# A hybrid token mixer whose projections run as matmuls of 512 columns, with PSUM handed out in pairs

## Chip, cores and metric

One NeuronCore of a Trainium2 chip (trn2). The time is device microseconds for one execution of the whole program. Of the kernel before, three runs are shown: median 2222.65 us, from 2222.18 to 2224.79 us. The profile is of one further execution, which took 2221.16 us.

## What is computed

Two layers over 256 latent tokens and 256 context tokens of width 1024, all in fp32. Cut to what matters here:

```python
for l in range(2):
    # half-step SwiGLU feed-forward (inner width 2816) on latent and context tokens
    x  = add_residual(x,  swiglu(modulate(x)),  0.5); xc = add_residual(xc, swiglu(modulate(xc)), 0.5)
    h, hc = modulate(x), modulate(xc)                 # RMSNorm, scale, shift
    rq, rk, rv, rg, dq, dk, dv, gates = split(h @ w_in)   # 8192 columns; the same for hc
    ret  = groupnorm(retention(rq, rk, rv)) * silu(rg)          # 4 heads, chunks of 128, state from context
    a    = softmax(dq1 @ dk1.T / 8) - lam * softmax(dq2 @ dk2.T / 8)  # 8 heads, keys of context and latent
    diff = rmsnorm(a @ dv) * (1 - lam_init)
    y    = (sigmoid(gates_a) * ret + sigmoid(gates_b) * diff) @ w_out
    x = add_residual(x, y, 1.0)       # the context too, except in the last layer
    # second half-step feed-forward, like the first; in the last layer for the latent tokens alone
```

The queries and keys of the latent tokens are rotated by position first. In the last layer the context needs no queries, gates or output, only keys and values.

## The kernel before

**Three matmuls for one.** Each large operand is kept as a high part (rounded to the short fp32r form) and a low part (the rest). `mm3` (lines 288 to 291) makes a product of them with three TensorE matmuls: high by high, high by low, low by high. A weight piece of 128x1024 arrives by DMA in a `raw` buffer (4 of them, issued in order by SP). `split` (lines 113 to 118) makes the parts: ScalarE casts the high one (line 116), VectorE subtracts for the low one (line 117), into one of five `w` buffers. The modulation weights (`ada`) are multiplied on VectorE (line 134), during the feed-forwards.

**The mixer** (line 397) takes the 8192 columns of `w_in` in 32 blocks of 256. A block's weights fill two `w` buffers. Rotated queries and keys are made with channels on partitions (`projT_c`, line 471: the weights stand in the array, 256 tokens of one condition stream past), everything else with tokens on partitions (`proj_c`, line 445: 128 tokens stand, 256 channels stream). "Condition" is latent (`LAT`) or context (`CTX`); each has 256 tokens. So every one of these matmuls has 256 columns and each PSUM bank takes two of them.

**The attention** is a generator (`diff_attn`, line 580) run in steps beside the projections. A step makes a score: four matmuls (lines 594 and 595), VectorE maxima (596), ScalarE exponentials (602), VectorE reciprocal, scaling and difference (605 to 609). Two steps later the result is transposed on TensorE (621), copied by ScalarE (623) and multiplied by the values (626). Retention (`ret_head`, line 681) runs the same way. `tick` (line 422) says how many steps follow each projection, `need` (line 433) drains a generator.

**What sets the order.** Each engine runs its instructions in one order, which a scheduler fixes when the program is built, from the order of the code and the readiness that it assumes. TensorE waits where the next instruction's data are late, even if later ones could run. PSUM is 8 banks of 512 columns, each a tile of its own, handed out in turn (`Ring`, line 54). A second ring has 15 SBUF slots of 4 KB per partition.

Of the kernel before, what the change touches and what calls it, by code (L numbers as in the profile page):

```python
# [29 lines left out]
LAG = 2  # L30


def build(ctx, tc, a):
# [8 lines left out]
    adap = ctx.enter_context(tc.tile_pool(name="adap", bufs=4))  # L42
# [25 lines left out]
    banks = Ring(psp, "ps", 8)  # L68
    slots = Ring(rp, "r", 15)

    def bank():
        return banks.get([P, 512])
# [32 lines left out]
    def load(src, halves=(0, 1), pl=rawp, nm="raw"):  # L105
        rs = []
        for j in halves:
            r = pl.tile([P, 1024], F32, tag=nm, name=nm)
            nc.sync.dma_start(r, src[:, j * 1024:(j + 1) * 1024])
            rs.append(r)  # L110
        return rs
# [16 lines left out]
    def ada_gen(l, m, out, conds):  # L128
        for u in range(4):
            r = load(a["wada"][l, m * 4 + u], pl=adap, nm="ada")  # L130
            for j in range(2):
                for c in conds:
                    junk = jp.tile([P, D], BF16, tag="jd", name="jd")
                    dve.tensor_tensor_reduce(  # L134
                        out=junk, in0=r[j], in1=cs[c],
                        scale=1.0, scalar=0.0, op0=ALU.mult, op1=ALU.add,
                        accum_out=out[:, c, 2 * u + j:2 * u + j + 1])
            yield
# [258 lines left out]
    def mixer(l, st, AB, fetch, after):  # L397
# [7 lines left out]
        o, y, M = {}, {}, {}  # L405
# [35 lines left out]
        def proj_w(b):  # L441
            r = load(a["win"][l, b])
            return [split(r[0]), split(r[1])]

        def proj_c(ws, c, ev):
            b0 = bank()
            bk = b0.rearrange("p (j n) -> p j n", j=2)
            for j in range(2):
                t = 2 * c + j
                for k in range(KD):  # L450
                    wt = ws[k // 4].rearrange("p s (k n) -> p s k n", k=4)
                    mm3(bk[:, j], h[k // 2][:, k % 2, 0, t * P:(t + 1) * P], h[k // 2][:, k % 2, 1, t * P:(t + 1) * P],
                        wt[:, 0, k % 4], wt[:, 1, k % 4], k == 0, k == KD - 1)
            flush()
            post = ev(c, bk)
            banks.put(b0)
# [4 lines left out]
        def proj(b, pairs, ev):  # L461
            ws = proj_w(b)
            for c in pairs:
                proj_c(ws, c, ev)

        def projT(b, pairs, ev):
            ws = proj_w(b)
            for c in pairs:
                projT_c(ws, c, ev)

        def projT_c(ws, c, ev):
            b0 = bank()
            bk = b0.rearrange("p (j n) -> p j n", j=2)
            cs_ = slice(c * 256, (c + 1) * 256)
            for j in range(2):
                js = slice(j * P, (j + 1) * P)
                for k in range(KD):
                    wt = ws[k // 4].rearrange("p s (k n) -> p s k n", k=4)
                    mm3(bk[:, j], wt[:, 0, k % 4, js], wt[:, 1, k % 4, js], h[k // 2][:, k % 2, 0, cs_],
                        h[k // 2][:, k % 2, 1, cs_], k == 0, k == KD - 1)  # L480
            flush()
            ev(c, bk)
# [36 lines left out]
        def ev_V(dst):  # L519
            def ev(c, b):  # L520
                nc.scalar.copy(dst[:, 2 * c:2 * c + 2, :], b)
            return ev

        def ev_V2(H, Lo):
            def ev(c, b):
                nc.scalar.copy(H[:, 2 * c:2 * c + 2, :], b)
                dve.tensor_tensor(out=Lo[:, 2 * c:2 * c + 2, :], in0=b, in1=H[:, 2 * c:2 * c + 2, :], op=ALU.subtract)
# [52 lines left out]
        def diff_attn(u, KH, KL, Q, dv):  # L580
            lag = deque()

            def score(c, k0, NK, t, hh):
                if c == LAT:
                    sbk = [bank(), bank()]
                    sb = sbk
                else:
                    b0 = bank()
                    sbk = [b0]
                    sb = [b0[:, 0:256], b0[:, 256:512]]  # L590
                mx = small(2, "mx")
                for m in range(2):
                    qs = Q[m][:, hh, t * P:(t + 1) * P]
                    mm(sb[m], lhsT=qs, rhs=KH[m][:, hh, k0:k0 + NK], start=True, stop=False)  # L594
                    mm(sb[m], lhsT=qs, rhs=KL[m][:, hh, k0:k0 + NK], start=False, stop=True)  # L595
                    dve.reduce_max(mx[:, m:m + 1], sb[m], axis=AX.X)  # L596
# [4 lines left out]
                for m in range(2):  # L601
                    act(e[:, m, :NK], sb[m], AF.Exp, bias=nb[:, m:m + 1], scale=0.125, accum_out=se[:, m:m + 1])  # L602
                banks.put(*sbk)
# [11 lines left out]
            def weigh(c, k0, NK, tt, hh, e):  # L615
# [9 lines left out]
                for i in range(NK // P):  # L625
                    mm(ob[:, tt, hh * P:(hh + 1) * P], lhsT=aT[:, i * P:(i + 1) * P],  # L626
                       rhs=dv[:, k0 // P + i, hh * P:(hh + 1) * P], start=i == 0, stop=i == NK // P - 1)
# [7 lines left out]
                if u not in o:  # L635
                    o[u] = slot([P, 4, 256])
                for tt in range(2):
                    for hh in range(2):
                        dve.scalar_tensor_tensor(out=o[u][:, 2 * c + tt, hh * P:(hh + 1) * P],
# [16 lines left out]
            slots.put(*KH, *KL, *Q, dv)  # L656
# [24 lines left out]
        def ret_head(hd, W, gnb, kk, qq, vv):  # L681
            hl = hd % 2
            for c in QP:
# [20 lines left out]
                if hd not in y:  # L704
                    y[hd] = slot([P, 4, 256])
                yt = y[hd]
                y0 = bank()
                yb = y0.rearrange("p (i n) -> p i n", i=2)
                for i in range(2):
                    for n, j in enumerate(kt):  # L710
                        an = AT[n // 2][:, :, n % 2, i * P:(i + 1) * P]
                        mm3(yb[:, i], an[:, 0], an[:, 1], vv[0][:, j], vv[1][:, j], n == 0, n == len(kt) - 1)
                st = small(12, "bst").rearrange("p (i s) -> p i s", i=2)
                mv = small(4, "bmv").rearrange("p (i s) -> p i s", i=2)
                for i in range(2):
# [6 lines left out]
                    dve.scalar_tensor_tensor(out=yt[:, t, :], in0=yb[:, i],  # L722
# [4 lines left out]
            slots.put(*vv)  # L727
            if hl:
                slots.put(*kk, *qq)

        def ev_gB(u):
            def ev(c, b):
                th = tmp2([P, 2, 256])
                act(th, b, AF.Tanh, scale=0.5)
                oc = o[u][:, 2 * c:2 * c + 2]
# [3 lines left out]
        def ev_rg(hd):  # L739
            def ev(c, b):  # L740
                th = tmp2([P, 2, 256])
                act(th, b, AF.Tanh, scale=0.5)
                dve.scalar_tensor_tensor(out=th, in0=th, scalar=1.0, in1=b, op0=ALU.add, op1=ALU.mult)
                for j in range(2):
                    t = 2 * c + j
                    ys = y[hd][:, t]
                    dve.scalar_tensor_tensor(out=ys, in0=ys, scalar=gr[:, t, hd:hd + 1],
                                             in1=th[:, j], op0=ALU.mult, op1=ALU.mult)
            return ev

        def ev_gA(u):
            def ev(c, b):
                th = tmp2([P, 2, 256])
                act(th, b, AF.Tanh, scale=0.5)
                dve.scalar_tensor_tensor(out=th, in0=th, scalar=1.0, in1=y[u][:, 2 * c:2 * c + 2], op0=ALU.add, op1=ALU.mult)
                dve.tensor_tensor(out=th, in0=th, in1=o[u][:, 2 * c:2 * c + 2], op=ALU.add)

                def post():
                    t0 = bank()
                    tb = t0.rearrange("p (k n) -> p k n", k=2)  # L760
                    for j in range(2):
                        for z in range(2):
                            nc.tensor.transpose(tb[:, z, j * P:(j + 1) * P], th[:, j, z * P:(z + 1) * P], ident)
                    for z in range(2):
                        mt = M[2 * u + z]
                        mH = mt[:, 0, c * 256:(c + 1) * 256]
                        nc.scalar.copy(mH, tb[:, z])
                        dve.tensor_tensor(out=mt[:, 1, c * 256:(c + 1) * 256], in0=tb[:, z], in1=mH, op=ALU.subtract)
                    banks.put(t0)
# [3 lines left out]
        def diff_blocks(u):  # L773
# [239 lines left out]
```

## Time and profile before

| | before |
|---|---|
| median of three runs | 2222.65 us |
| the profiled execution's own time | 2221.16 us |
| its span, first to last instruction | 2219.4 us |
| TensorE matmul busy | 2171.0 us (98%) |
| VectorE busy | 1381.9 us (62%) |
| ScalarE busy | 863.1 us (39%) |

Matmul records overlap: each lasts from its first column to the modelled end of its drain, and the next one starts before. So a matmul's cost in a dense stretch is read from the distance of two starts, not from the duration of a record. Idle time is counted only where no matmul record covers it. The mixers run from about 408 to 928 us and from about 1662 to 2014 us; the rest is feed-forward, a start of some 55 us, and norms.

### The profile page before, as it was taken

To read this page: it belongs to the slowest core of one execution; us is meant where nothing else is said; L and a number is where in the kernel's file an instruction comes from. 1 tells how busy PE (TensorE), PEld (TensorE's weight loads), DVE (VectorE), ACT (ScalarE), POOL (GpSimd) and SP (SyncE) were. 2 spreads that over 40 slices of the span, in tenths; PEclk is the share of its full clock that TensorE was granted. 3 is DMA by queue.
4 is the path that set the end of the run, shared out by engine and by line. 5 is a ranking of instruction groups with operands and counts; after the bars stand their busy time and mean duration, and the time that the engine had idled before them with its cause. 6 is when DMAs were issued, how large, how long until landed. Compare 5 with 4: busy or idle time off the path is not lost. (4 is left out here: it accounts for less than half of the span.)

```text
span 2219.4 us, 32920 instructions
## 1 busy us (share of the span) xinstructions
PE 2171.0 (98%) x13286; PEld 1932.7 (87%) x13286; DVE 1381.9 (62%) x2240; ACT 863.1 (39%) x1379; POOL 127.6 (6%) x245
## 2 busy tenths in 40 slices
PE   7999999999999999999999999999999999998998
PEld 4888888899999999888888888888879999997997
DVE  3899442777767664588234269844348777767554
ACT  3322232645355433432223252223236545445443
POOL 1000000200100010200000020000011010001000
PEclk9999999999999999999999999999999999999999
DMA  8677332122122223266223227853213322345553
GB/s 338 216 253 254 132 121 97 68 70 80 66 77 77 80 85 117 76 209 218 97 102 134 95 92 254 296 184 116 102 57 113 107 84 103 132 152 184 187 184 133
DMA packets 85417, 307.33 MB, mean 138 GB/s; under 512 B 10208, under 2 KB 10416, under 8 KB 85264
## 3 DMA queue, kind: packets, MB, share of 16 engines
q1 hardware_dynamic: 82224, 295.87, 38.1%
q0 software_dynamic: 2752, 8.31, 1.3%
q8 instruction: 104, 1.70, 0.3%
q10 hardware_dynamic: 288, 1.05, 0.1%
q14 instruction: 49, 0.40, 0.1%
HBM read 304.10 MB, written 1.09 MB: 138 GB/s over the span
## 5 line engine op out<-in xcount | busy, mean ns | idle before, releaser
L117 DVE TENSOR_TENSOR w<-raw,w 128x1024 fp32r<-128x1024 f32 x408 | 497.7, 1222 | 462.6 <-ACT w L116 461.5
L289 PE MATMUL ps<-h,w 128*128 128x256 f32 (+1 forms) x2176 | 716.9, 331 | 3.7 <-DVE h L254 2.9
L291 PE MATMUL ps<-h,w 128*128 128x256 f32 (+1 forms) x2176 | 717.3, 330 | 0.4 <-DVE w L117 0.4
L290 PE MATMUL ps<-h,w 128*128 128x256 f32 (+1 forms) x2176 | 717.5, 330 | 0.0
L116 ACT CAST w<-raw 128x1024 fp32r<-128x1024 f32 x408 | 427.5, 1052 | 684.7 <-PE ps L291 613.3
L289 PEld LDWEIGHTS ps<-h,w 128*128 128x128 f32 x2176 | 412.1, 190 | 43.2 <-DVE h L254 4.0
L291 PEld LDWEIGHTS ps<-h,w 128*128 128x128 f32 x2176 | 412.8, 190 | 41.0 <-issue 2.5
L290 PEld LDWEIGHTS ps<-h,w 128*128 128x128 f32 x2176 | 413.3, 190 | 40.1 <-DVE w L117 0.8
L289 PE MATMUL ps<-w,h 128*128 128x256 f32 x1088 | 308.8, 284 | 0.0
L290 PE MATMUL ps<-w,h 128*128 128x256 f32 x1088 | 308.1, 283 | 0.0
L291 PE MATMUL ps<-w,h 128*128 128x256 f32 x1088 | 307.8, 283 | 0.0
L134 DVE CUSTOM_DVE_ANT_0 jd<-ada,r 128x1024 bf16<-128x1024 f32 x224 | 273.6, 1221 | 15.4 <-DMA ada<-wada_dram 10.4
L289 PEld LDWEIGHTS ps<-w,h 128*128 128x128 f32 x1088 | 208.7, 192 | 0.4
L290 PEld LDWEIGHTS ps<-w,h 128*128 128x128 f32 x1088 | 208.7, 192 | 0.3
L291 PEld LDWEIGHTS ps<-w,h 128*128 128x128 f32 x1088 | 208.6, 192 | 0.0
L289 PE MATMUL ps<-w,gs 128*128 128x512 f32 x504 | 196.2, 389 | 0.0
L290 PE MATMUL ps<-w,gs 128*128 128x512 f32 x504 | 196.1, 389 | 0.0
L291 PE MATMUL ps<-w,gs 128*128 128x512 f32 x504 | 196.1, 389 | 0.0
L315 ACT ACTIVATE t<-ps 128x512 f32<-128x512 f32 (+1 forms) x88 | 47.9, 544 | 253.2 <-PE ps L291 249.8
L316 DVE TENSOR_TENSOR r<-ps,t 128x512 f32<-128x512 f32 (+1 forms) x88 | 54.7, 622 | 95.3 <-PE ps L291 69.6
L289 PEld LDWEIGHTS ps<-w,gs 128*128 128x128 f32 x504 | 94.6, 188 | 19.8
L290 PEld LDWEIGHTS ps<-w,gs 128*128 128x128 f32 x504 | 94.6, 188 | 19.6
(169 smaller groups left out, 2164.6 us busy)
## 6 DMA issues: line engine op xcount, KB each, us to landing
raw<-fin_dram SPq DMA_DIRECT2D x176, 512.0 KB, 4.2
ada<-wada_dram SPq DMA_DIRECT2D x128, 512.0 KB, 4.8
raw<-win_dram SPq DMA_DIRECT2D x128, 512.0 KB, 3.5
raw<-fout_dram SPq DMA_DIRECT2D x88, 512.0 KB, 3.5
r<-wada_dram SPq DMA_DIRECT2D x16, 512.0 KB, 10.2
raw<-wout_dram SPq DMA_DIRECT2D x16, 512.0 KB, 3.6
r<-scr POOLq DMA_DIRECT2D x10, 512.0 KB, 4.7
r<-cc_dram SPq DMA_DIRECT2D x7, 512.0 KB, 5.1
```

The costliest lines, as they stand in the source:

```text
L116: keep(nc.scalar.copy(w[:, 0, :], src))
L117: keep(dve.tensor_tensor(out=w[:, 1, :], in0=src, in1=w[:, 0, :], op=ALU.subtract))
L134: dve.tensor_tensor_reduce(out=junk, in0=r[j], in1=cs[c], scale=1.0, scalar=0.0, op0=ALU.mult, op1=ALU.add, accum_out=out[:, c, 2 * u + j: ...
L289: mm(o, lhsT=wH, rhs=xH, start=start, stop=False)
L290: mm(o, lhsT=wH, rhs=xL, start=False, stop=False)
L291: mm(o, lhsT=wL, rhs=xH, start=False, stop=stop)
L315: act(sg[:, :N], ab[0][:, :N], AF.Silu)
L316: dve.tensor_tensor(out=g[f // 2][:, f % 2, :N], in0=ab[1][:, :N], in1=sg[:, :N], op=ALU.mult)
```

## The change

The blocks become 12 of 256 columns with channels on partitions (`winT`) and 10 of 512 columns with tokens on partitions (`winW`). `projT` takes both conditions in one matmul of 512 columns, into two neighbouring banks; `wide` streams 512 channels past 128 tokens, so that it needs four `w` buffers at once. PSUM is one tile; `Banks` hands out single banks or pairs. A latent score takes a pair, and one instruction takes its two maxima. The modulation weights lose their own four buffers and use the slot ring, now 19. `ret_decay` moves into the generator. The stage order is written anew: values of heads 0 and 1 first, then keys and queries of two attention blocks one after the other.

```diff
+    def two(self): ...  # a pair of neighbouring banks; one(): a single one, of an opened pair
-    banks = Ring(psp, "ps", 8)
-    slots = Ring(rp, "r", 15)
+    banks = Banks()
+    slots = Ring(rp, "r", 19)
...
-            r = load(a["wada"][l, m * 4 + u], pl=adap, nm="ada")
+            r = [slot([P, D]) for _ in range(2)]
...
-        def proj_c(ws, c, ev):
-            b0 = bank()
-            bk = b0.rearrange("p (j n) -> p j n", j=2)
-            for j in range(2):
-                t = 2 * c + j
-                for k in range(KD):
-                    wt = ws[k // 4].rearrange("p s (k n) -> p s k n", k=4)
-                    mm3(bk[:, j], h[k // 2][:, k % 2, 0, t * P:(t + 1) * P], h[k // 2][:, k % 2, 1, t * P:(t + 1) * P],
-                        wt[:, 0, k % 4], wt[:, 1, k % 4], k == 0, k == KD - 1)
+        def tok(ws, t, ev):
+            bk = bank()
+            for k in range(KD):
+                wt = ws[k // 2].rearrange("p s (k n) -> p s k n", k=2)
+                mm3(bk, h[k // 2][:, k % 2, 0, t * P:(t + 1) * P], h[k // 2][:, k % 2, 1, t * P:(t + 1) * P],
+                    wt[:, 0, k % 2], wt[:, 1, k % 2], k == 0, k == KD - 1)
+            flush()
+            post = ev(t, bk)
...
+        def wide_w(i):
+            return [split(r) for r in load(a["winW"][l, i], range(4))]
...
+            ws = [split(r) for r in load(a["winT"][l, b])]
+            n = 256 * len(pairs)
+            if len(pairs) == 2:
+                b0 = banks.two()
...
+                    mm3(bk[:, j], wt[:, 0, k % 4, js], wt[:, 1, k % 4, js], h[k // 2][:, k % 2, 0, 0:n],
+                        h[k // 2][:, k % 2, 1, 0:n], k == 0, k == KD - 1)
...
+            for c in pairs:
+                ev(c, bk[:, :, c * 256:(c + 1) * 256])
...
-                    sbk = [bank(), bank()]
+                    b0 = banks.two()
...
-                    dve.reduce_max(mx[:, m:m + 1], sb[m], axis=AX.X)
+                dve.reduce_max(mx, sb, axis=AX.X)
...
+        ws = wide_w(4)
+        for t in range(2):
+            tok(ws, t, ev_V(dv))
+        norm_pair(CTX, AB, h)
+        for t in range(2, 4):
+            tok(ws, t, ev_V(dv))
+        K.update(mixer_consts())
+        kq = diff_blocks(0)
+        diff_defer(0, kq, dv, pick(5, 4))
+        kq = diff_blocks(1)
+        diff_defer(1, kq, dv, pick(6, 5))
+        need("d0")
         rkq_blocks(0)
-        need("d0")
-        diff_blocks(1)
-        gB_block(0)
-        rv_block(0)
+        rv_block(0, pick(4, 2), pick(8, 5))
         need("d1")
-        rv_block(1)
-        gB_block(1)
+        wide(8, QP, ev_gB(0))
+        kq = diff_blocks(2)
...
```

The scheduler makes a new order of it. Three places are shown.

**TensorE, layer 0, first attention block, before.** L594 and L595 are a score's matmuls, L289 to L291 a projection's, L621 the transposition of the first score.

```order
L594 MATMUL ps_3603<-r_3047,r_3051 128x512
L595 MATMUL ps_3603<-r_3049,r_3051 128x512
L594 MATMUL ps_3623<-r_3046,r_3050 128x512
L595 MATMUL ps_3623<-r_3048,r_3050 128x512
...
L289 MATMUL ps_3644<-h,w 128x256
L290 MATMUL ps_3644<-h,w 128x256
L291 MATMUL ps_3644<-h,w 128x256
...
L594 MATMUL ps_3708<-r_3047,r_3051 128x512
L595 MATMUL ps_3708<-r_3049,r_3051 128x512
L621 MATMUL ps_3696<-ident,t_3613 128x128 x4
```

**The same place in the change** (L635 and L636 are the score's matmuls, L328 to L330 the projection's, L662 the transposition).

```order
L635 MATMUL ps<-r_3201,r_3287 128x512
L636 MATMUL ps<-r_3203,r_3287 128x512
L636 MATMUL ps<-r_3202,r_3286 128x512
...
L329 MATMUL ps<-h,w 128x512
L330 MATMUL ps<-h,w 128x512
L328 MATMUL ps<-h,w 128x512
...
L635 MATMUL ps<-r_3200,r_3286 128x512
...
L662 MATMUL ps<-ident,t_3408 128x128 x4
```

Between the last matmul of the first score and its transposition stood 48 projection matmuls of 256 columns and 8 score matmuls; now 14 of 512 columns and 7 score matmuls stand there.

**TensorE, layer 1, first attention block, in the change**, from the first score's last matmul.

```order
L636 MATMUL ps<-r_12477,r_12561 128x512
L635 MATMUL ps<-r_12474,r_12560 128x512
...
L329 MATMUL ps<-h,w 128x512
L330 MATMUL ps<-h,w 128x512
L328 MATMUL ps<-h,w 128x512
...
L662 MATMUL ps<-ident,t_12678 128x128 x4
```

Here 5 projection matmuls and 8 score matmuls are left between the two; before it were 48 and 8, as in layer 0.

**VectorE, start of the mixer in layer 0, in the change.** L317 and L323 are the last residual of the feed-forward, L153 the low parts of weights, L275 the context's norm.

```order
L317 TENSOR_TENSOR t_2956<-ps,r_2743 128x512
L153 TENSOR_TENSOR w<-raw,w 128x1024
L317 TENSOR_TENSOR t_2960<-ps,r_2743 128x512
L323 SCALAR_TENSOR_TENSOR X_107<-t_2956,pr,X_107 128x512
L323 SCALAR_TENSOR_TENSOR X_107<-t_2960,pr,X_107 128x512
L153 TENSOR_TENSOR w<-raw,w 128x1024 x2
L275 TENSOR_SCALAR t_3052<-X_106,pr 128x1024
```

VectorE's order here is as before; but the last two low parts now belong to the first block on TensorE, where before they belonged to the second.

## Rows read from the trace of the kernel before

**Rows 1.** The page's line of engines: busy us, share of the span, instructions.

```profile
PE 2171.0 (98%) x13286; PEld 1932.7 (87%) x13286; DVE 1381.9 (62%) x2240; ACT 863.1 (39%) x1379; POOL 127.6 (6%) x245
```

**Rows 2.** The page's 40 slices of the span (55 us each): busy share in tenths, and TensorE's granted clock in tenths.

```profile
PE   7999999999999999999999999999999999998998
DVE  3899442777767664588234269844348777767554
PEclk9999999999999999999999999999999999999999
```

**Rows 3.** Matmuls of the whole span grouped by line and shape: busy us, mean ns of a record, idle time before them and its releaser. `mm3` issues one of L289, L290, L291 each; `ps<-h,w` streams `h`, `ps<-w,h` streams weights.

```profile
L289 PE MATMUL ps<-h,w 128*128 128x512 f32 x960 | 373.9, 389 | 0.0
L289 PE MATMUL ps<-h,w 128*128 128x256 f32 x1216 | 343.3, 285 | 3.7 <-DVE h L254 2.9 <-ACT t L251 0.6 <-DVE adaA L921 0.2
L289 PE MATMUL ps<-w,h 128*128 128x256 f32 x1088 | 308.8, 284 | 0.0
```

**Rows 4.** TensorE in order of time, in a projection of the mixer: start us, duration us. The rows left out are 45 more of the same three lines.

```profile
641.71 0.28 PE L289 MATMUL ps<-w,h 128*128 128x256 f32 x1
641.82 0.28 PE L290 MATMUL ps<-w,h 128*128 128x256 f32 x1
...
647.34 0.28 PE L291 MATMUL ps<-w,h 128*128 128x256 f32 x1
```

**Rows 5.** TensorE in order of time, in a feed-forward: start us, duration us. The rows left out are 43 more.

```profile
299.68 0.39 PE L289 MATMUL ps<-w,gs 128*128 128x512 f32 x1
299.91 0.39 PE L290 MATMUL ps<-w,gs 128*128 128x512 f32 x1
...
309.88 0.39 PE L289 MATMUL ps<-w,gs 128*128 128x512 f32 x1
```

**Rows 6.** TensorE's waits in the attention, whole span, grouped by line and shape (columns as in group 3).

```profile
L621 PE MATMUL ps<-ident,t 128*128 128x128 f32 x160 | 25.0, 274 | 3.5 <-DVE t L609 3.4
L626 PE MATMUL ps<-r,t 128*128 128x128 f32 x320 | 45.5, 284 | 1.5 <-ACT t L623 1.0
```

**Rows 7.** Busy us of each engine in stretches: a feed-forward, and the first attention block of either layer's mixer. Columns: stretch in us, its length; busy us and instructions of PE, PEld, DVE, ACT, POOL; mean granted clock, DMA's busy share, GB/s.

```profile
100.00:150.00 50.00, 50.00 (x223) 41.29 (x222) 49.45 (x82) 12.60 (x14) 0.53 (x1) 1.00 0.73 250
450.00:500.00 50.00, 48.93 (x386) 46.51 (x385) 38.44 (x89) 21.76 (x53) 2.44 (x4) 1.00 0.19 64
1700.00:1750.00 50.00, 49.33 (x397) 47.78 (x396) 43.27 (x88) 26.75 (x47) 2.17 (x3) 1.00 0.25 87
```

**Rows 8.** Start of the mixer in layer 0, in order of time: TensorE, then VectorE. In brackets the idle time before it and its releaser.

```profile
408.18 0.39 PE L291 MATMUL ps<-w,r 128*128 128x512 f32 x1
408.40 0.28 PE L289 MATMUL ps<-h,w 128*128 128x256 f32 x1
416.50 0.63 PE L247 MATMUL ps<-ident,t 128*128 128x128 f32 x4 [0.86 <-DVE t L236]
426.40 0.51 PE L289 MATMUL ps<-h,w 128*128 128x256 f32 x2 [1.78 <-DVE h L254]
...
412.53 2.35 DVE L117 TENSOR_TENSOR w<-raw,w 128x1024 fp32r<-128x1024 f32 x2
419.78 0.75 DVE L236 TENSOR_SCALAR t<-X,pr 128x1024 f32<-128x1024 f32 x1
425.92 0.43 DVE L254 CAST h<-t 128x512 fp32r<-128x512 f32 x1 [1.68 <-ACT t L251]
```

**Rows 9.** TensorE, layer 0, first attention block: the last matmul of the first score, and the transpositions of the first and the fourth.

```profile
454.88 0.40 PE L595 MATMUL ps<-r,r 128*128 128x512 f32 x1
...
462.92 0.66 PE L621 MATMUL ps<-ident,t 128*128 128x128 f32 x4
...
473.56 0.60 PE L621 MATMUL ps<-ident,t 128*128 128x128 f32 x4
```

**Rows 10.** TensorE, a later attention block: the last matmul of its first score and that score's transposition.

```profile
640.56 0.40 PE L595 MATMUL ps<-r,r 128*128 128x512 f32 x1
...
647.46 0.60 PE L621 MATMUL ps<-ident,t 128*128 128x128 f32 x4
```

**Rows 11.** VectorE from 405 to 2040 us, grouped by line and shape (columns as in group 3).

```profile
L117 DVE TENSOR_TENSOR w<-raw,w 128x1024 fp32r<-128x1024 f32 x284 | 346.1, 1221 | 314.5 <-ACT w L116 313.5
L491 DVE TENSOR_TENSOR t<-ps,dtab 32x512 f32<-32x512 f32 x64 | 44.0, 687 | 1.0
L596 DVE TENSOR_REDUCE mx<-ps 128x1 f32<-128x512 f32 x64 | 42.0, 682 | 10.4 <-PE ps L595 10.3
L608 DVE TENSOR_SCALAR t<-t,rc 128x512 f32<-128x512 f32 x32 | 15.4, 480 | 0.0
L609 DVE SCALAR_TENSOR_TENSOR t<-t,r 128x512 f32<-128x512 f32 x32 | 24.0, 749 | 0.8
L663 DVE TENSOR_SCALAR gnb<-gnb 128x256 f32<-128x256 f32 x8 | 2.3, 289 | 7.9 <-DMA gnb<-gnw_dram 7.9
```

**Rows 12.** ScalarE's cast of weights, same stretch and columns.

```profile
L116 ACT CAST w<-raw 128x1024 fp32r<-128x1024 f32 x284 | 297.1, 1051 | 458.3 <-PE ps L291 413.8 <-issue 33.6 <-DVE adag L134 4.4
```

**Rows 13.** Stretches around TensorE's longest idle time, in the last layer between mixer and feed-forward (columns as in group 7).

```profile
2016.00:2020.00 4.00, 0.00 (x0) 0.00 (x0) 3.01 (x5) 3.20 (x9) 3.56 (x6) 0.91 0.39 133
2020.00:2024.00 4.00, 1.78 (x7) 1.41 (x8) 2.46 (x3) 0.00 (x0) 2.28 (x3) 0.50 0.35 114
2024.00:2028.00 4.00, 4.00 (x27) 3.94 (x27) 2.60 (x6) 3.75 (x8) 0.00 (x0) 0.74 0.06 24
```

More of the change, by code (lines that the diff above doesn't have):

```diff
@@ L66, in put, with __init__, one, two @@
                 self.free.append(self.of.pop(id(t))[0])
-    banks = Ring(psp, "ps", 8)
-    slots = Ring(rp, "r", 15)
+    psum = psp.tile([P, 8, 512], F32, tag="ps", name="ps")
+    class Banks:
+        def __init__(self):
+            self.pairs, self.halves, self.of, self.age, self.n = deque(range(4)), [], {}, [0] * 8, 0
+        def one(self):
+            if not self.halves or (len(self.pairs) > 1 and max(self.age[2 * self.pairs[0]], self.age[2 * self.pairs[0] + 1])
+                                   < min(self.age[i] for i in self.halves)):
+                p = self.pairs.popleft()
+                self.halves += [2 * p, 2 * p + 1]
+            i = min(self.halves, key=lambda z: self.age[z])
+            self.halves.remove(i)
+            b = psum[:, i]
+            self.of[id(b)] = (b, i, 1)
+            return b
+        def two(self):
+            p = self.pairs.popleft()
+            b = psum[:, 2 * p:2 * p + 2]
+            self.of[id(b)] = (b, 2 * p, 2)
+            return b
+        def put(self, *bs):
+            for b in bs:
+                _, i, n = self.of.pop(id(b))
+                for z in range(i, i + n):
+                    self.n += 1
+                    self.age[z] = self.n
+                    if z ^ 1 in self.halves:
+                        self.halves.remove(z ^ 1)
+                        self.pairs.append(z // 2)
+                    else:
+                        self.halves.append(z)
+    banks = Banks()
+    slots = Ring(rp, "r", 19)
     def bank():
-        return banks.get([P, 512])
+        return banks.one()
     def slot(shape, dt=F32):
@@ L137, in ada_gen @@
                         accum_out=out[:, c, 2 * u + j:2 * u + j + 1])
+            slots.put(*r)
             yield
@@ L655, in diff_attn @@
                 yield
-            slots.put(*KH, *KL, *Q, dv)
+            slots.put(*KH, *KL, *Q)
+            if u % 2:
+                slots.put(*dv)
         def ret_decay(hd):
@@ L758, in post @@
                 def post():
[L759 to L768, printed above, removed]
@@ new lines, in pick @@
+        def pick(both, lat):
+            return lat if last else both
+        dv = [slot([P, 2, 512]) for _ in range(2)]
+        ws = wide_w(4)
[10 more added lines that the diff above has]
+        need("d0")
@@ L846, in mixer @@
+        need("r3")
+        for c in QP:
+            for j in range(2):
+                rg_y(1, 2 * c + j, rgs[c][:, j])
+            slots.put(rgs[c])
+        wide(7, QP, ev_gA(1))
         flush()
```

231 lines of the change are left out of this document (116 added, 115 removed).

## The prediction

> **What bounds the kernel now.** I read the line of engines first: TensorE is busy 2171.0 of 2219.4 us, 98%, VectorE 62%, ScalarE 39% [rows 1]. Then the 40 slices: TensorE stands at 9 in nearly all of them, in the mixers too, and the clock never leaves 9 [rows 2]. So the time is the sum of TensorE's matmuls plus little idle time, and two questions decide: how many microseconds of matmul the change takes away, and where TensorE then waits for something that is covered today.
>
> The price of a matmul comes from distances of starts, since records overlap. In a projection 47 steps between matmuls of 256 columns take 647.34 − 641.71 = 5.63 us, 0.120 us each [rows 4]. In a feed-forward 45 steps of 512 columns take 309.88 − 299.68 = 10.20 us, 0.2267 us each [rows 5]. Two of 256 cost 0.240 us, one of 512 costs 0.2267: 13.3 ns are won for every pair that becomes one.
>
> The attention is where idle time would grow. TensorE waits 3.5 us before transpositions and 1.5 us before products with the values, 5.0 us in all [rows 6]: today the chain from a score to its transposition is just covered. VectorE, which carries much of that chain, is busy 38.4 of 50 us in layer 0's first attention block and 43.3 of 50 in layer 1's [rows 7].
>
> **Wider matmuls.** The rows count 1216 matmuls of 256 columns with `h` standing and 1088 with weights standing, per line of `mm3` [rows 3]. In the order of the change 640 of the former are left on a line and none of the latter. So 3 × (576 + 1088) = 4992 matmuls go and half as many, 2496, of 512 columns come. They cost 4992 × 0.120 = 599.0 us now, 2496 × 0.2267 = 565.8 us then: **−33.2 us**, all of it on the engine that bounds. Would a matmul of 512 columns cost more in the mixer than in a feed-forward? The feed-forward ones run with TensorE 50.00 of 50 us busy and VectorE at 41 of 50 [rows 7], as loaded as a mixer, so I keep the price.
>
> Between the two pitches lie 226.7 − 120.0 = 106.7 ns for 256 columns more, so a matmul of 256 has 13.3 ns that don't depend on its columns, and these are what a pair saves [rows 4, 5]. A page speaks against a saving of this size: the Trainium skill, "TensorE: Matmul & The Clock Gate", section "Wait — 56ns, not 53.3ns?", gives a warm back-to-back matmul a fixed extra of about 2.5 ns, whatever its columns; by it the change would save an estimated 2496 × 2.5 ns = 6 us. The trace does not agree with it: it has 13.3 ns where the page has 2.5 [rows 4, 5].
>
> **Start of a mixer.** The first block now needs four weight tiles. The last two low parts are done on VectorE at 412.53 + 2.35 = 414.9 us, the first of them at 413.7 [rows 8]. TensorE starts the mixer at 408.4 and has 23 matmuls, 5.2 us, before the third tile's low part: up to 413.6. That costs 0.1 us. Then the context's norm: TensorE idles 0.86 us before its transpositions and 1.78 before the first matmul on the result [rows 8]. Now 48 matmuls of 512 columns, 10.9 us, stand ahead of the transpositions, about the time that is needed, and one wait of about 1.3 us is left: −1.5 us a layer, **−3 us** in both. Bounds: the two waits gone (−2.6 a layer, about −5 in all), or one late split a layer, 1.05 for the cast [rows 12] and 1.22 for the low part [rows 11], +2.3 each, about +4 in all.
>
> **Attention, by the new order.** Between a score's last matmul and its transposition stood 48 × 0.120 + 8 × 0.227 = 7.6 us of TensorE work. What the chain needs: a later block went from 640.56 to 647.46 without idle time, so its 6.9 us are a ceiling [rows 10]; the VectorE pieces alone are 2 × 0.68 (maxima), 0.48 and 0.75 us, 2.6, without the exponentials and hand-overs [rows 11]. I take 6.3, near the ceiling, since that row is the same chain. In the crowded first block it took 8.0 us (454.88 to 462.92), and 18.7 us to the fourth transposition (473.56) [rows 9].
> - Layer 0, first attention block: 14 + 7 matmuls, 4.8 us, are left. The first transposition is 8.0 − 4.8 = 3.2 us short. Up to the fourth stand 11.4 us of work, at most 18.7 − 11.4 = 7.3 short. The middle: +5.3.
> - Layer 1, first block: 5 + 8 matmuls, 2.95 us: 6.3 − 2.95 = +3.35. Layer 1, last block: 3.3 us left, +3.0. The third block in either layer: 5.0 us left, +1.3 each. The other three keep 6.4 us or more: 0.
>
> Sum **+14.2 us**. Bounds: nothing (the chain is faster when nothing crowds it), or 8.0 us of chain everywhere and 7.3 in layer 0: 7.3 + 5.05 + 4.7 + 2 × 3.0 = +23. Why a wait may be long: keys and queries of two attention blocks now follow each other with no values between. A block of them costs VectorE 10 rotations at 0.69 and 2 low parts at 1.22, 9.3 us [rows 11], against 48 × 0.2267 = 10.9 us on TensorE. That leaves 1.6 us a block for the attention's own VectorE work, of which a score alone needs 2.6.
>
> **The rest.** One maximum over two banks takes the place of two at 0.68 us [rows 11]; no row shows it, its price lies between 0.68 and 1.36, and I take 1.36, its elements being as many; at 0.68 it takes some 0.7 us from a chain, up to −3 us in the tight places. The modulation weights wait for slots of the ring instead of buffers of their own. They run beside feed-forwards in which TensorE is 50.00 of 50 busy and VectorE 41 [rows 7]: 0; without that cover one late tile costs 1.05 + 1.22 = 2.3 us [rows 11, 12]. `ret_decay` and its loads move past the first projections on POOL's queue; VectorE waits 7.9 us for these loads today, eight times, with TensorE not idle for it [rows 11]: 0, between −1 and +1 us a head at most. SP issues as many weight loads as before. An eviction now starts when both conditions are done, so a pair of banks is held 10.9 us and the eviction; the order gives the next block another pair, 0.
>
> **Sum**: 2221.2 − 33.2 − 3 + 14.2 = 2199.2 us against the profiled execution. The median of the runs is 1.5 us above that execution, so about 2200.7; I say **2200 us**.
>
> **Rivals.**
> 1. The waits don't grow: the chain is quicker than I take it, and the scheduler's shorter fill suffices. 2221.2 − 33.2 − 3 = 2185, as a median 2186.5. For it: the 6.9 us are only a ceiling [rows 10]. Against it: 2.95 us of work can't cover a chain whose VectorE pieces alone are 2.6 [rows 11].
> 2. VectorE becomes the bound of the attention stretches. It is at 43.3 of 50 us in one [rows 7]. If the four stretches that begin with two blocks of keys and queries run at its pace, each adds some 4 to 5 us to the forecast, all four 16: 2216, between 2208 and 2222. Against it: the later values and gates leave VectorE room, which TensorE uses only where its order lets it.
> 3. Slower: the weight buffers. A `wide` block holds four of the five, so the next one's second tile can be split only when the last 128 tokens are 6 matmuls in, and is needed 6 matmuls into the next block, 24 × 0.2267 = 5.45 us later. Cast and low part take 2.27 [rows 11, 12], the slack is 3.2 us. With one score's 2.6 us ahead on VectorE it holds; with two, 5.2, it is 2.0 us short. At all 20 such blocks that is +40 us, about 2240. It decides if it happens at 12 blocks or more (24 us beyond the forecast is no change). For it: VectorE waits for a cast 313.5 us in all, so splits are made as late as buffers come free [rows 11]. Against: only a few wide blocks have scores beside them so densely.
> 4. The change gives little of what it promises: the 13.3 ns lie in something other than the number of matmuls, and 512 columns in the mixer cost nearly two times 256, 0.2375 instead of 0.2267 us. Then 6 of the 33 us are left, 2221.2 − 6 − 3 + 14.2 = 2226.4, as a median 2228. Against: [rows 5] has the price in 45 steps. The page named above would have about this time too, by its smaller fixed part.
>
> A side risk in all of them is the clock. When TensorE stood still from before 2016 to past 2020 us, the granted clock was 0.50 in the next 4 us and 0.74 in the 4 after, 1.2 GHz of 2.4 for part of the time [rows 13]: some 2 + 1 = 3 us lost. Waits as long as that I expect in none of the blocks.
>
> **How the numbers follow.** Forecast 0.50; rival 1 0.22; rival 2 0.16; rival 3 0.07; rival 4 0.02; anything else 0.03. Range 2184 to 2220: from rival 1 with 2.5 us more to the bulk of rival 2; it takes in +23 for the attention (2209) and, on top, late splits and lost cover. Outside lie rivals 3 and 4, the end of rival 2 and the tail below rival 1, about 0.2. A measurement tells about 0.2% from no change, here 4.4 us: 2218.2 to 2227.1 is the same. Faster: 0.50 + 0.22 + 0.10 of rival 2 = 0.82. Same: 0.06 of rival 2, half of rival 4 and most of the rest, 0.10. Slower: 0.08.
>
> **What would show it.** Right: projection matmuls 0.227 us apart, TensorE's busy time lower by about 33 us and its idle time higher by 10 to 15, nearly all before the transposition's line and the product with the values, most of it in layer 0's first attention block. Wrong: steps of 0.235 us or more (rival 4); idle time before the weights' lines at starts of blocks (rival 3); VectorE at 48 of 50 us in an attention stretch with TensorE idle through it (rival 2); idle time in the attention still near 5 us (rival 1); a clock below 1 in a mixer.

## The result, and the profile after

The changed kernel takes 2237.19 us (median of 4 runs, 2235.81 to 2241.39) beside 2223.72 us of the kernel before on the same chip: ratio 1.0065, 95% interval 1.0052 to 1.0077. It is slower by 13 us, where 23 us less were forecast, and it lies outside the range. The profiled execution has a span of 2234.0 us. Of the runs below, one of halves (2454 us, granted clock 0.83) and one of the kernel before (4348 us) lie far off the others and are not in the ratios.

The page of the changed kernel: engines, then 40 slices of the span (as in [rows 1, 2]).

```profile
PE 2150.8 (96%) x10790; PEld 1803.2 (81%) x10790; DVE 1378.1 (62%) x2180; ACT 865.8 (39%) x1367; POOL 128.5 (6%) x245
PE   7999999979999999999999999999998999898998
DVE  3897362677667764596243389635257676677454
PEclk9999999999999999999999999999999999999999
```

TensorE is busy 20 us less and the span is 15 us longer, so it stands idle 83 us instead of 48. The clock's row shows nothing: a slice is 56 us, and each fall of the clock here lasts some 10. Lines of TensorE by shape (as in [rows 3, 6]):

```profile
L328 PE MATMUL ps<-h,w 128*128 128x512 f32 x1248 | 488.9, 392 | 7.4 <-ACT t L643 7.4
L328 PE MATMUL ps<-w,h 128*128 128x512 f32 x544 | 212.6, 392 | 3.7 <-ACT t L643 3.1 <-DVE h L293 0.6
L328 PE MATMUL ps<-h,w 128*128 128x256 f32 x640 | 181.6, 288 | 1.8 <-ACT t L290 1.0 <-DVE h L293 0.5 <-DVE adaA L976 0.2
L668 PE MATMUL ps<-r,t 128*128 128x128 f32 x320 | 46.6, 288 | 3.9 <-ACT t L664 3.5
L662 PE MATMUL ps<-ident,t 128*128 128x128 f32 x160 | 26.3, 282 | 8.5 <-DVE t L650 8.5
```

What TensorE waited for in the projections and the attention, by line and releaser: us in all, times, longest. Rows of norms, modulation and retention are left out, here and in the lists of the runs below.

```profile
PE ps L635 <- DVE r L553: 11.4, 6, 5.1
PE ps L328 <- ACT t L643: 10.5, 5, 6.3
PE ps L662 <- DVE t L650: 8.5, 6, 3.1
PE ps L635 <- ACT t L643: 8.1, 2, 6.1
PE ps L668 <- ACT t L664: 3.5, 7, 0.7
PE ps L328 <- DVE h L293: 1.2, 4, 0.3
PE ps L329 <- DVE w L153: 0.6, 1, 0.6
PE ps L330 <- DVE w L153: 0.4, 2, 0.2
```

L553 makes the low part of queries and keys (of the latent ones after their rotation), L643 is a score's exponential, which gives its PSUM banks back, L650 and L664 are the chain to the transposition and the values. The first, second and fourth of these rows, 30 us, have nothing that answers to them in [rows 6].

To set gains against losses I split each span in two. **Lost time** is, over all steps from one matmul's start to the next, what the step takes beyond the full-clock pitch of its shape (0.227 us at 512 columns, 0.120 at 256, 0.109 at 128), where that is over 15 ns: waits and half clock together. The **rest** is the matmul work.

| kernel | span | lost time | rest | median |
|---|---|---|---|---|
| before | 2219.4 | 73.6 | 2145.8 | 2223.7 |
| changed | 2234.0 | 119.5 | 2114.5 | 2237.2 |
| dense (before, steps due sooner) | 2246.7 | 102.5 | 2144.2 | 2246.9 |
| singles | 2236.4 | 121.3 | 2115.1 | 2237.2 |
| narrow | 2238.8 | 114.7 | 2124.1 | 2243.6 |
| late | 2247.6 | 133.2 | 2114.4 | 2250.4 |
| halves | 2223.9 | 109.1 | 2114.8 | 2228.3 |
| even | 2238.2 | 123.4 | 2114.8 | 2239.8 |
| even_narrow | 2220.8 | 95.8 | 2125.0 | 2223.4 |
| even_halves | 2221.1 | 107.0 | 2114.1 | 2228.5 |
| even_late | 2204.0 | 88.9 | 2115.1 | 2206.7 |
| even_late_halves | 2202.0 | 88.1 | 2113.9 | 2204.5 |
| even_late_narrow | 2204.9 | 79.6 | 2125.3 | 2207.2 |
| mix | 2198.1 | 84.1 | 2114.0 | 2199.2 |

The names are those of the experiments below. The first three columns are of one profiled execution each; in halves and even_halves that was the fastest of the runs, 2.6 and 5.6 us under the median.

The matmul work fell by 31.3 us; the lost time rose by 45.9. The layers differ. From the first transposition of the norm ahead of a mixer to the first one of the norm behind it, the first layer takes 516.2 us after 519.3 before, the last layer 386.8 after 368.2: lost time rose from 25.0 to 40.3 us in the first and from 18.4 to 48.4 in the last. So the whole loss of the span lies in the last layer's mixer, which has fewer matmuls to put between the steps (the context has no queries there); that this is the reason is not shown. Outside the mixers the span fell by 0.9 us, so the modulation weights' way through the slot ring shows no cost.

Two places show how time is lost. First ScalarE, then VectorE, then TensorE of the changed kernel, layer 0, in order of time (start, duration; idle time before and its releaser in brackets).

```profile
478.10 0.62 ACT L551 CAST r<-t 64x512 fp32r<-64x512 f32 x1 [0.87 <-DVE t L533]
478.74 0.62 ACT L555 CAST r<-t 64x512 fp32r<-64x512 f32 x1
...
481.22 1.87 ACT L556 CAST r<-r 64x512 fp32r<-64x512 f32 x3
483.10 0.58 ACT L551 CAST r<-ps 64x512 fp32r<-64x512 f32 x1
483.71 0.69 ACT L643 ACTIVATE t<-ps,nb 128x512 f32<-128x512 f32 x1
484.39 0.68 ACT L643 ACTIVATE t<-ps,nb 128x512 f32<-128x512 f32 x1
```

```profile
476.12 1.22 DVE L637 TENSOR_REDUCE mx<-ps 128x2 f32<-128x1024 f32 x1
478.58 0.15 DVE L639 TENSOR_SCALAR nb<-mx 128x2 f32<-128x2 f32 x1
```

```profile
478.16 0.28 PE L636 MATMUL ps<-r,r 128*128 128x256 f32 x1
484.54 0.58 PE L635 MATMUL ps<-r,r 128*128 128x256 f32 x1 [6.10 <-ACT t L643]
```

The maxima of a latent score are scaled on VectorE at 478.6 (L639). Its exponential (L643) is queued on ScalarE behind the eviction of a block of keys for both conditions, copies of 0.6 us each from 478.10 to 483.68, and starts at 483.71. Only then does a bank come free, and the next score, which waits for it, starts at 484.54 after 6.1 us of idle time. The longest wait of the mixers, in the last layer, is of the same kind: the maxima are scaled at 1727.1, eight more copies of an eviction run on ScalarE up to 1732.1, then comes the exponential, and then the projection that waits for its bank.

```profile
1727.12 0.15 DVE L639 TENSOR_SCALAR nb<-mx 128x2 f32<-128x2 f32 x1
1732.13 0.69 ACT L643 ACTIVATE t<-ps,nb 128x512 f32<-128x512 f32 x1
1732.96 0.79 PE L328 MATMUL ps<-h,w 128*128 128x512 f32 x1 [6.34 <-ACT t L643]
```

These two are 12.4 of the 18.6 us that hang on L643. The waits of 1.6 us at 653 and 1863 us are not of this kind: there ScalarE was idle too, and waited for VectorE's maxima.

The second place is TensorE at the start of layer 0's fourth attention block (the rows left out are 22 more of L328 to L330):

```profile
704.33 0.39 PE L328 MATMUL ps<-w,h 128*128 128x512 f32 x1
...
709.54 0.39 PE L330 MATMUL ps<-w,h 128*128 128x512 f32 x1
715.07 0.80 PE L635 MATMUL ps<-r,r 128*128 128x512 f32 x1 [5.14 <-DVE r L553]
```

The queries' last matmul started at 704.10. One stretch of 24 matmuls follows, 5.45 us, then the first score waits 5.14 us for them to be rotated and split: they are ready 11 us after their last matmul started. In the kernel before a block of values stood between.

The longest waits cost once more (stretch, its length; busy us of PE, PEld, DVE, ACT, POOL; granted clock, DMA):

```profile
480.00:484.00 4.00, 0.00 (x0) 0.00 (x0) 1.43 (x3) 3.91 (x7) 0.00 (x0) 0.82 0.38 131
484.00:488.00 4.00, 3.41 (x14) 2.93 (x14) 2.74 (x7) 2.36 (x6) 0.00 (x0) 0.50 0.00 0
1716.00:1720.00 4.00, 2.02 (x7) 1.21 (x6) 3.56 (x8) 1.72 (x6) 0.00 (x0) 0.50 0.35 126
1728.00:1732.00 4.00, 0.00 (x0) 0.00 (x0) 0.69 (x1) 3.93 (x7) 0.00 (x0) 0.56 0.00 0
1732.00:1736.00 4.00, 2.98 (x10) 2.26 (x11) 2.17 (x5) 2.75 (x7) 0.00 (x0) 0.50 0.00 0
```

The granted clock is 0.50 in the 4 us after the wait that ended at 484.54 and around the one that ended at 1732.96, 1.2 GHz of 2.4. It is 0.50 from 1716 to 1720 us too, behind and beside two waits of 2.0 us each. Over the mixers in stretches of 4 us, TensorE's busy time multiplied by what the clock lacks of 1 sums to 13.4 us, in the kernel before to 1.9.

### The profile page after: what moved, and what is told of

It is laid out like the page before. It is cut to its first block, busy times and chain, and to the rows that moved or that the text cites. A ratio compares the mean times of both kernels' runs of the same rounds, so it can differ in the third digit from the quotient of the medians.

```text
span 2234.0 us, 27800 instructions
## 1 busy us (share of the span) xinstructions
PE 2150.8 (96%) x10790; PEld 1803.2 (81%) x10790; DVE 1378.1 (62%) x2180; ACT 865.8 (39%) x1367; POOL 128.5 (6%) x245
## 5 line engine op out<-in xcount | busy, mean ns | idle before, releaser
L153 DVE TENSOR_TENSOR w<-raw,w 128x1024 fp32r<-128x1024 f32 x408 | 497.7, 1222 | 451.4 <-ACT w L152 447.4
L328 PE MATMUL ps<-h,w 128*128 128x512 f32 (+1 forms) x1888 | 670.2, 356 | 9.2 <-ACT t L643 7.4
L329 PE MATMUL ps<-h,w 128*128 128x512 f32 (+1 forms) x1888 | 669.2, 355 | 0.0
L330 PE MATMUL ps<-h,w 128*128 128x512 f32 (+1 forms) x1888 | 668.6, 355 | 0.4 <-DVE w L153 0.4
L328 PEld LDWEIGHTS ps<-h,w 128*128 128x128 f32 x1888 | 358.3, 190 | 60.5 <-ACT t L643 8.3
L330 PEld LDWEIGHTS ps<-h,w 128*128 128x128 f32 x1888 | 358.5, 190 | 52.4 <-issue 3.4
L329 PEld LDWEIGHTS ps<-h,w 128*128 128x128 f32 x1888 | 359.2, 190 | 47.4
L172 DVE CUSTOM_DVE_ANT_0 jd<-r,r 128x1024 bf16<-128x1024 f32 x224 | 273.3, 1220 | 5.6 <-ACT r L162 1.0
L328 PE MATMUL ps<-w,h 128*128 128x512 f32 x544 | 212.6, 392 | 3.7 <-ACT t L643 3.1
L329 PE MATMUL ps<-w,h 128*128 128x512 f32 x544 | 212.7, 392 | 0.6 <-DVE w L153 0.6
L330 PE MATMUL ps<-w,h 128*128 128x512 f32 x544 | 212.3, 391 | 0.0
L328 PE MATMUL ps<-w,gs 128*128 128x512 f32 x504 | 196.2, 389 | 0.0
L330 PE MATMUL ps<-w,gs 128*128 128x512 f32 x504 | 196.1, 389 | 0.0
L328 PEld LDWEIGHTS ps<-w,h 128*128 128x128 f32 x544 | 102.2, 188 | 25.2 <-ACT t L643 4.0
L355 DVE TENSOR_TENSOR r<-ps,t 128x512 f32<-128x512 f32 (+1 forms) x88 | 54.7, 622 | 107.0 <-PE ps L330 80.0
L329 PEld LDWEIGHTS ps<-w,h 128*128 128x128 f32 x544 | 102.3, 188 | 21.8 <-DVE w L153 2.2
L330 PEld LDWEIGHTS ps<-w,h 128*128 128x128 f32 x544 | 102.2, 188 | 20.5
L328 PEld LDWEIGHTS ps<-w,gs 128*128 128x128 f32 x504 | 94.6, 188 | 19.9
L330 PEld LDWEIGHTS ps<-w,gs 128*128 128x128 f32 x504 | 94.6, 188 | 19.6
```

The costliest lines, as they stand in the source:

```text
L153: keep(dve.tensor_tensor(out=w[:, 1, :], in0=src, in1=w[:, 0, :], op=ALU.subtract))
L172: dve.tensor_tensor_reduce(out=junk, in0=r[j], in1=cs[c], scale=1.0, scalar=0.0, op0=ALU.mult, op1=ALU.add, accum_out=out[:, c, 2 * u + j: ...
L328: mm(o, lhsT=wH, rhs=xH, start=start, stop=False)
L329: mm(o, lhsT=wH, rhs=xL, start=False, stop=False)
L330: mm(o, lhsT=wL, rhs=xH, start=False, stop=stop)
L355: dve.tensor_tensor(out=g[f // 2][:, f % 2, :N], in0=ab[1][:, :N], in1=sg[:, :N], op=ALU.mult)
```

## The experiments

Theories. **A, density**: the new order runs three attention steps after one projection of 24 matmuls, where two followed 48 of 256 columns; VectorE and ScalarE don't keep up. **B, burst**: evictions for both conditions come at once. **C, pairs**: a score holds a pair of four. **D, distance**: the first score stands too near to its queries; it came up with the first results. Each ratio below is to the kernel before on the same chip in the same round (medians of 2222.6 to 2224.3 us). Every edit is also scheduled anew, so that more moves than the lines shown; the waits are read beside the times for that reason.

**even**: another stage order with the same blocks.

```diff
-        diff_defer(0, kq, dv, pick(5, 4))
-        kq = diff_blocks(1)
-        diff_defer(1, kq, dv, pick(6, 5))
-        need("d0")
+        diff_defer(0, kq, dv, pick(8, 7))
         rkq_blocks(0)
-        rv_block(0, pick(4, 2), pick(8, 5))
-        need("d1")
-        wide(8, QP, ev_gB(0))
+        rv_block(0, 4, 6)
+        need("d0")
+        ...  # values of heads 2, 3
+        need("r1")
+        kq = diff_blocks(1)
+        diff_defer(1, kq, dv, pick(6, 4))
...
```

> The changed kernel with all its matmuls, pairs and evictions, but another stage order: each attention block's steps are spread over 6 to 8 later projections (4 in the last layer at times) instead of over the 3 to 4 of the next keys and queries. Theory A (density: three attention steps per 24 matmuls, 5.45 us, are more than VectorE and ScalarE can take beside the evictions): most of the 37 us that TensorE waits in the attention and of the some 12 us at half clock go, 2190 to 2205 us. Theory B (two-condition evictions come as bursts of some 7 us on ScalarE and VectorE, ahead of the attention's work): the bursts stay, 2225 us or more. Theory C (a latent score holds a pair of banks, and there are only four): 2225 us or more.

2239.79 us, ratio to the kernel before 1.0074 (1.0059 to 1.0089): no gain. TensorE's waits in it:

```profile
PE ps L635 <- DVE r L553: 28.9, 8, 5.7
PE ps L662 <- DVE t L650: 3.7, 3, 2.0
PE ps L328 <- ACT t L643: 3.5, 4, 1.6
PE ps L635 <- ACT t L643: 2.6, 2, 2.0
PE ps L668 <- ACT t L664: 1.0, 2, 0.7
```

Density did what A says: the waits for banks and chain fell from 30.6 us to 10.8. But the first row went from 11.4 to 28.9: five first scores now stand 24 matmuls behind their queries and wait 4.5 to 5.7 us each, where the changed kernel has one (5.14 us). A alone is not enough, and 2239.79 us lies in the figures that were given for B and C.

**narrow**: `projT` goes over the conditions one by one, with `bank()`, 256 columns and an eviction for each condition.

> The changed kernel and its stage order, but blocks with channels on partitions are done one condition at a time again (256 columns, one bank, an eviction for each condition); the wide blocks stay. 3264 matmuls of 256 columns come back for 1632 of 512, +21.7 us of TensorE. Theory A: the waits stay as they are, 2250 to 2262 us. Theory B: waits and half clock fall by 25 us or more, 2225 to 2238 us. Theory C: projections take no pairs any more, some 10 us of waits go, 2240 to 2250 us.

2243.60 us (1.0077 to 1.0108). The 21.7 us are wrong, and the theories' figures with them: that share belongs to the wide blocks, and what came back are 1728 matmuls for 864, 864 × 13.3 ns = 11.5 us (the rest column shows 9.6). By the right price A has 2240 to 2252 us and B 2215 to 2228, and the time is A's: lost time fell by 4.8 only. An eviction for one condition at a time gains little in an order as dense as this one; an eviction by bank gains more (halves, below).

**singles**: `bs = [bank(), bank()]` and a `reduce_max` for each, in place of `banks.two()`.

> The changed kernel, but a latent score takes two single banks and two maxima, as before the change. Theory C: the waits for exponentials to give banks back (some 19 us) mostly go, 2212 to 2222 us. Theories A and B: the waits move to other places, 2228 to 2243 us; two maxima of 0.68 us for one of 1.2 add up to 3 us of that.

2237.24 us (1.0046 to 1.0079), lost time 121.3 against 119.5. C falls: with single banks the waits for L643's counterpart are 11.9 us instead of 18.6, and others turn up, above all 10.7 us of one transposition behind a block's copies (L555).

**dense**: the kernel before with one number changed.

```diff
-            defer(f"d{u}", diff_attn(u, KH, KL, Q, dv), 2 * NQ + 3, 4 * NQ + LAG)
+            defer(f"d{u}", diff_attn(u, KH, KL, Q, dv), NQ + 3, 4 * NQ + LAG)
```

> The kernel before with one number changed: an attention block's steps are due within NQ + 3 projections (5, in the last layer 4) instead of 2 NQ + 3 (7 and 5). Matmuls, banks and evictions are those of before. Theory A: three steps follow one projection here too, TensorE's waits in the attention grow by 10 to 25 us, 2233 to 2248 us. Theories B and C: their causes are absent, 2222 to 2227 us.

2246.92 us (1.0093 to 1.0126), +24 us, as A has it. The kernel before, which had no such row, now waits where the changed one does, a projection (L289) for the exponential (L602):

```profile
PE ps L289 <- ACT t L602: 16.9, 8, 3.3
```

No wide matmul, pair or joint eviction is in this kernel's mixers. Density alone adds 28.9 us of lost time, 63% of the 45.9 that the change added; the time is longer than the changed kernel's since no matmul work was saved against it.

**even_late**: `tick` does nothing until a block's start, one tick after `defer`; due times 8, 8, 8, 8 (last layer 7, 6, 6, 6; in even 8, 6, 6, 8 and 7, 4, 4, 5). So where even was due within 6 or 4, the three steps behind the first projection become two: the run adds distance and takes some density away as well.

```diff
-            if sideq:
+            if sideq and clock[0] >= sideq[0][4]:
...
-            sideq.append([gen, clock[0] + within, steps + 1, key])
+            sideq.append([gen, clock[0] + within, steps + 1, key, clock[0] + 1 + skip])
```

> The even stage order, and each attention block skips the first projection after its queries, so 48 matmuls of 512 columns (10.9 us) stand before its first score instead of 24; its steps are due within 8 projections (6 or 7 in the last layer). Theory D (distance: the rotated queries are ready some 10 us after their last matmul, and a score that stands nearer makes TensorE wait and lose its clock): the 28.9 us of waits for the rotation in the even order fall below 8, half clock with them, 2200 to 2215 us. Theory A alone (density): little changes, 2230 to 2242 us, since the steps get no sparser.

2206.73 us, ratio 0.9933 (0.9911 to 0.9954), 16 us under the kernel before and inside D's figures:

```profile
PE ps L635 <- ACT t L643: 3.5, 3, 2.7
PE ps L662 <- DVE t L650: 2.9, 5, 1.1
PE ps L668 <- ACT t L664: 2.0, 3, 0.7
PE ps L635 <- DVE r L553: 1.5, 2, 1.0
PE ps L328 <- ACT t L643: 1.1, 1, 1.1
```

The rotation's row fell from 28.9 to 1.5; half clock from 18.2 us in even to 7.0. That row is D's; how much of the rest is due to the later due times, no run separates.

**late**: the skip alone, in the changed kernel's order.

> The changed kernel in its own stage order, each attention block skips the first projection after its queries; the due times stay, so up to four steps follow one projection. Distance alone (D): the 11.4 us of waits for the rotation and some half clock go, 2218 to 2228 us. Density and distance both (A and D, each covering for the other): what is won at the rotation is lost behind denser steps, 2232 to 2250 us.

2250.42 us (1.011 to 1.014): up to four steps now follow one projection, and lost time rises to 133.2. The row of L553 falls from 11.4 to 6.1 us, but a score waits 13.0 us for a block's copies (L555) and two others 16.0 us in all for an exponential. Distance that is paid for with denser steps loses, sparser steps without distance gained nothing (even), both together take 31 us of lost time away.

**halves**: in `projT`, `ev(c, bk[:, j:j + 1, ...], j)` behind each bank's 24 matmuls, in instructions half as long and twice as many; **even_halves** is the same in the even order.

> The changed kernel in its own stage order, each bank of a block with channels on partitions evicted when its own 24 matmuls are done, in instructions half as long. Theory B: waits for the rotation (11.4 us) and part of those for banks behind the evictions (18.6 us) go, with half clock 15 to 25 us, 2212 to 2222 us. Theory A: density stays, 2230 to 2240 us.

> The even order without the skip, each bank of a block with channels on partitions evicted when its own 24 matmuls are done. If the waits of the even order come from the time between the queries' last matmul and their rotation (10 us) against 24 matmuls of cover (5.45 us), halving the burst brings the two close: the 28.9 us of waits fall below 8, 2203 to 2216 us. If the wait hangs on the place of the score alone and not on the burst: 2228 to 2240 us.

2228.28 us (1.0016 to 1.005) and 2228.51 us (1.0014 to 1.0033). Either is some 10 us faster than the same order with whole evictions. halves falls between the figures expected; even_halves lies at the lower end of the second ones, though its waits for the rotation fell to 7.1 us, as the first ones have it. Other waits took their place: projections wait 9.8 us for the exponential and 7.3 us for L531, a step of the rotation. halves has the latter too:

```profile
PE ps L328 <- DVE t L531: 7.0, 4, 2.9
```

These four waits are made by the edit itself: in the last layer the queries are of one condition and both groups of 24 matmuls write one bank, so that the second group stands until VectorE has rotated the first out of it. The changed kernel, even and late have no such row. B is a part of the cause in both orders, by more than the 10 us if that wait is left out of account, and not all of it.

**even_narrow**: one condition at a time in the even order.

> The even stage order without the skip, with one condition at a time in the blocks with channels on partitions (256 columns; +21.7 us of matmuls). The latent queries are evicted while the context's 48 matmuls run. Theories B and D: the waits for the rotation go, 28.9 us and some 8 us of half clock, 2218 to 2230 us. Theory A alone: 2255 to 2265 us.

2223.44 us (0.9995 to 1.0014): work +10.2 us, lost time −27.6 against even. The wait for the rotation is 1.2 us: the latent queries are evicted beside the context's 48 matmuls. It is inside the figures expected for B and D only by the wrong 21.7 us; by the right price of the matmuls they would have had 2208 to 2220 us, and it lies just above that, and far from A's figures.

**even_late_halves** and **even_late_narrow**:

> The same, and each bank of a block with channels on partitions is evicted when its own 24 matmuls are done, in instructions half as long (twice as many). Theory B (it is the burst of both conditions' evictions on ScalarE and VectorE that everything waits for): another 5 to 15 us go beyond even_late, 2190 to 2205 us. If distance and density have taken the waits already: within 4 us of even_late, or up to 10 us slower by the fixed cost of the additional instructions.

> The even order with the skip, one condition at a time in the blocks with channels on partitions: 3264 matmuls of 256 columns for 1632 of 512, +21.7 us, where hardly a wait is left to hide it: 2222 to 2230 us. If the price of 256 against 512 columns is not what the distances of starts say: 2205 to 2215 us.

even_late_halves takes 2204.52 us (0.9899 to 0.9931), within 4 us of even_late and with an interval that overlaps: no verdict between the two. By layers they differ: from transposition to transposition, as above, it is 501.4 us with evictions by bank and 509.7 without in the first layer, 370.1 and 363.2 in the last, where the edit's own wait on L531 costs 3.9 us.

even_late_narrow takes 2207.19 us (0.9914 to 0.9944). The expectation has the same wrong 21.7; with 11.5 it would be some 2218 us. The price of the matmuls is as computed (11.5 us; the rest column has +10.2), but lost time is 9.3 us lower: even where the order leaves room, lost time takes back nearly all that the two-condition matmuls win. That it is their joint evictions that do it is argued, since this edit changes banks and steps too. What stays is the wide blocks' 1632 × 13.3 ns = 21.7 us.

**mix**: even_late, with evictions by bank in the first layer and whole ones in the last.

> The even order with the skip; evictions by bank in the first layer, of whole blocks in the last. By the spans of the mixers in the two runs that it joins (501.4 us in the first layer with evictions by bank, 361.4 in the last without) 2195 to 2201 us. If a layer's time hangs on something other than its own evictions: 2203 to 2208 us.

2199.21 us, ratio 0.9898 (0.9881 to 0.9915): 1% under the kernel before, and as the two mixers' spans add up (501.4 and 364.3 us). Its interval overlaps that of even_late_halves and touches that of even_late, so that a gain over these is not shown by the times. Rows of its attention (L700 is its transposition, L593 an eviction's copy, L681 the exponential, L673 a score):

```profile
PE ps L700 <- DVE t L688: 5.5, 5, 2.6
PE ps L328 <- ACT r L593: 2.9, 3, 1.4
PE ps L328 <- ACT t L681: 1.9, 2, 1.1
PE ps L673 <- DVE r L558: 1.0, 1, 1.0
```

## Why the prediction was wrong, step by step

- **Wider matmuls, −33.2 us**: right; the rest column has −30.7 to −31.9 in every version with all wide and all two-condition blocks. The pitch of 512 columns holds in the mixer (704.33 to 709.54: 23 steps, 0.2265 us each), and rival 4 falls. By the Trainium skill, "TensorE: Matmul & The Clock Gate", section "Wait — 56ns, not 53.3ns?", with its fixed extra of about 2.5 ns a matmul, the saving was an estimated 6 us; the measurement decides against that here. The prediction named the two kinds the wrong way round (weights stand in the `h,w` ones); the sum has both and doesn't change.
- **Start of a mixer, −3 us**: right. The steps there lost 4.7 us before and about 1 us after; the waits for VectorE's last step of a norm (L293) are 1.2 us in the whole kernel, feed-forwards included.
- **Attention, +14.2 us**: right in kind, and half as large. The idle time before transpositions and values went from 5.0 us [rows 6] to 12.4 (8.5 and 3.9), +7.4. Layer 0's first attention block, which was to have most of it, has 3.3 us.
- **"a pair of banks is held 10.9 us and the eviction; the order gives the next block another pair, 0"**: this is the step that failed. It asked whether a bank was there, not when the exponential that frees it gets its turn on ScalarE. 18.6 us of waits hang on L643, for scores and for projections, against none on its counterpart before. singles shows that the pair is not the reason. The traces show a queue of copies ahead of the exponential for 12.4 us of it; dense, where such waits come up without the change, and even, where they fall to 6.1 us, show that they follow the density of the steps.
- **A term that was missing**: a score waits for its own queries, 11.4 us. The text saw that keys and queries now follow each other with no values between, and drew from it VectorE's load alone. The 11 us from the queries' last matmul to the rotated result were covered by the values block before and are not by 24 matmuls.
- **The clock**: waits "as long as that I expect in none of the blocks", but there were waits of 5.1 to 6.3 us, and half clock cost 13.4 − 1.9 = 11.5 us more in the mixers.

Sum by these: −31.3 − 3.7 + 7.4 + 18.6 + 11.4 + 11.5 = +13.9; the span grew by 14.6.

Rival 1 (the waits don't grow) falls with the waits above. Rival 2 (VectorE the bound) falls. In the stretches of [rows 7] it is busier in the kernel before than in the changed one:

```profile
450.00:500.00 50.00, 38.82 (x193) 31.08 (x192) 37.19 (x74) 30.12 (x66) 1.28 (x2) 0.93 0.13 42
1700.00:1750.00 50.00, 36.97 (x180) 29.43 (x178) 34.95 (x59) 27.94 (x50) 1.59 (x2) 0.83 0.16 54
```

VectorE is at 37.2 and 35.0 of 50 us, ScalarE at 30 and 28, with TensorE at 39 and 37. No engine is full over these stretches. Rival 3 (weight buffers) named the right sign and the wrong place: waits for weights are 1.0 us in all.

What stays open: how density, distance and burst share the 46 us exactly, since each covers for the others and no run changes one of them by itself in the changed kernel; why the last layer loses so much more than the first; and what more a stage order made for these evictions would give, with 84.1 us lost in mix against 73.6 in the kernel before.

## What to carry to other kernels

A wider matmul's saving reaches the span only where the work that it releases at once (evictions, and what queues behind them) still fits between two of its uses: price the queue ahead of the instruction that frees a bank, not the bank. When a block is moved out from between a producer and its consumer, compare the time from the producer's last matmul to the finished eviction with the matmuls that are left between. A mean busy share of 60 to 75% on the side engines says nothing about steps in clusters. And a wait can cost more than its length: here the half clock around the waits cost 11.5 us more than before.

## What the runs showed of the hardware

One maximum over two banks takes 1.216 us, two over one bank took 0.682 each [rows 11]:

```profile
L637 DVE TENSOR_REDUCE mx<-ps 128x2 f32<-128x1024 f32 x32 | 38.3, 1216 | 1.3 <-PE ps L636 1.0
```

So the merged one saves 0.15 us a score; the prediction took 1.36 us for it, the upper of its two bounds, and it lies nearer to that than to 0.68.
